# A seven-product block scheme for the second weight of two feed-forward layers

## The chip, the cores and the metric

One core of a Trainium2 chip runs the whole kernel as one program. The metric is the device time of one execution in microseconds. The kernel before took 1127.52 us (median of three runs, 1127.25 to 1127.96).

## What is computed

One layer of a streaming encoder for 512 tokens of width 1024, in float32: a feed-forward half step, a mixer (a recurrent branch and windowed attention), and a second feed-forward half step, with an RMS norm around each. The change touches the last product of the two feed-forward parts (FFNs).

```python
D_MODEL, SEQ, D_FF = 1024, 512, 2816

def rms_norm(x, g):
    y = x * lax.rsqrt(jnp.mean(x * x, axis=-1, keepdims=True) + RMS_EPS)
    return y * g

def swiglu(x, w1, w3, w2):
    return (jax.nn.silu(x @ w1) * (x @ w3)) @ w2

f = swiglu(rms_norm(h, ffn1_pre_g), ffn1_w1, ffn1_w3, ffn1_w2)
h = h + 0.5 * rms_norm(f, ffn1_post_g)
...                                    # the mixer
f = swiglu(rms_norm(h, ffn2_pre_g), ffn2_w1, ffn2_w3, ffn2_w2)
h = h + 0.5 * rms_norm(f, ffn2_post_g)
```

With `w2` the contraction runs over 2816 hidden channels, 22 tiles of 128. The result has 512 tokens (4 tiles of 128) by 1024 columns (2 halves of 512).

## The kernel before

**Numbers.** Every float32 operand is split into a high part (a copy to the matmul's float32r type) and a low part (what the copy lost). A product takes three matmuls: high by high, high by low, low by high. The copy to the high part runs on ACT (ScalarE), the subtraction for the low part on DVE (VectorE); `split2` (L211) is the pair. `split_dma` (L154) makes a low part without DVE: ACT writes the negated high part, and a transfer issued by POOL (GpSimd) adds the operand to it in place.

**Order.** The order of instructions on each engine is the order in which the program issues them; nothing is rearranged. `later(n, fn)` and `point()` (L197, L201) put a piece of work n steps further on. A list `order` (L102) holds the order in which weights are loaded; `dma_to`, `split_to` and `get` (L149, L164, L183) load, split and hand out the next ones. All weight loads go through SP's queue. Tiles in SBUF come from one pool of 42 equal slots of 4 KB per partition (`slot`, L63); the eight PSUM banks from another (`bank`, L67).

**w1 and w3** of an FFN already run in a seven-product block scheme (`Pairs`, L522), a job for two tiles of one weight, 84 matmuls of 256 columns each. At two places in its last job `Pairs.run` calls `tail()`, which prepares the start of what follows. In the first FFN the hidden tiles 2 and 3 are kept unscaled (`keep`, `gate_kept`, `swiglu_kept`) and finished after the jobs. `Hidden` holds the hidden tiles, and `Hidden.to` splits them.

**w2** runs in `tok_gemm` (L360, also used for `wo`): the tokens are the stationary operand, 512 columns of the weight are moving, and eight PSUM banks hold the whole result (four token tiles, two column halves). The first F = 15 contraction tiles go tile by tile over all tokens; the last RF = 7 are kept back and go token by token, so that each token tile is finished in turn, and its norm (`post_norm`, `norms`, L284, L308) runs while PE (TensorE) goes on. In the first FFN the tokens are then transposed (L331) for the mixer, while PE begins the next product on the first half of the tokens (L433 to L468). In the second FFN the result goes out. POOL has nothing to do in the w2 stages but to issue the loads of the norm gains and to scale one.

Of the kernel before, what the change touches and what calls it, by code (L numbers as in the profile page):

```python
# [51 lines left out]
def hybrid_layer(ctx: ExitStack, tc: tile.TileContext, a: dict, out: bass.AP):  # L52
# [50 lines left out]

    def want(name, n):
        order.extend((name, i) for i in range(n))

# [10 lines left out]
    want_ffn("w1a", "w3a", NC1)  # L117
    want("w2a", FT)
    order += [("xr", i) for i in range(8)]
# [14 lines left out]
    want_ffn("w1b", "w3b", NC2)  # L134
    want("w2b", FT)

# [146 lines left out]

    def post_norm(acc, t, gpost, scale, dst, after=None, last=False, eps=D * EPS, mid=None):  # L284

        ss = small(2, "ss")
        fg = slot([P, D], name="fg")
        junk = slot([P, D], name="junk")
        cs = [slice(n * 512, (n + 1) * 512) for n in range(2)]
        rs = Rstd2()  # L290
        for n, c in enumerate(cs):
            act.activation(junk[:, c], acc[n], AF.Square, accum_out=ss[:, n : n + 1])
            dve.scalar_tensor_tensor(out=fg[:, c], in0=acc[n], scalar=scale, in1=gpost[:, c], op0=ALU.mult, op1=ALU.mult)
            if n:
                rs.root(ss)
            else:
                rs.first(ss, eps)
        r = rs.value()
        if mid:
            mid()  # L300
        if last:
            cs = [slice(0, 512), slice(512, 768), slice(768, D)]
        for n, c in enumerate(cs):
            dve.scalar_tensor_tensor(out=dst[:, c], in0=fg[:, c], scalar=r, in1=h[t][:, c], op0=ALU.mult, op1=ALU.add)
            if after:
                after(n, c)

    def norms(acc, t, gpost, scale, gpre, spill, eps, mid=None):  # L308
# [12 lines left out]
        post_norm(acc, t, gpost, scale * NEWT, h[t], half, eps=eps, mid=mid)  # L321
# [37 lines left out]

    def tok_gemm(nm, xs, n, R, gpost_name, scale, gpre_name, first, x_to=None, xf=None, spill=False, then=None, eps=None):  # L360

# [11 lines left out]

        pre = min(2, F)
        x_to = x_to or (lambda k: None)
        for k in range(pre):
            x_to(k + 1)
            w[k] = get(nm, k, ahead=pre - k + 1)
        if pre:
            for tt in ((0, 1), (2, 3)):  # L380
                for k in range(pre):
# [4 lines left out]
        for k in range(pre, F):  # L386
            x_to(k + 2)
            w[k] = get(nm, k, ahead=2 + (R - 2) * (k + 1) // F)
            for t in range(NT):
                mm_tok(accs(t), xs[k], t, w[k], k == 0, False)  # L390
                if t % 2:
                    point()
        point(True)
        for k in range(F, n):
            x_to(k + 1)
            w[k] = get(nm, k, ahead=max(0, n - 1 - k), rawahead=2)
# [8 lines left out]
        for t in range(NT):  # L405
            for ns in ((0,), (1,)):
                for k in range(F, n):
                    mm_tok(accs(t), xs[k], t, w[k], k == 0, k == n - 1, ns)
            if not gpre_name:
                o = slot([P, D], name="o")  # L410

                def store(nn, c, t=t, o=o):
                    sp.dma_start(out=out[t * P : (t + 1) * P, c], in_=o[:, c])

                post_norm(acc[t], t, gpost, scale * NEWT, o, store, t == NT - 1)
# [8 lines left out]
            us[t] = norms(acc[t], t, gpost, scale, gpre, spill, ep(t))  # L424
            if t == 1:
                transpose_out(trs[t - 1], t - 1, xf)
# [19 lines left out]
        mm_feat(bs[0], ws[0], 0, 256, ks=range(3, KT))  # L446
        us[t] = norms(acc[t], t, gpost, scale, gpre, spill, ep(t), between)
        transpose_out(trs[t - 1], t - 1, parts=(1,))
# [24 lines left out]

    def silu_mul(ps1, ps3, t=None):

        t = t or slot([P, 2, SEQ], name="sw")
        act.activation(t[:, 0, :], ps1, AF.Silu)
        dve.tensor_tensor(out=t[:, 1, :], in0=ps3, in1=t[:, 0, :], op=ALU.mult)
        return t[:, 1, :]

    class Hidden:


        def __init__(self):
            self.f, self.t, self.done = [], {}, 0

        def to(self, n):
            while self.done < min(n, len(self.f)):
                assert self.f[self.done] is not None
                hT = slot([P, 2, SEQ], F32R, name="hT")  # L490
                split2(hT[:, 0, :], hT[:, 1, :], self.f[self.done])
                self.f[self.done] = None
                self.t[self.done] = hT
                self.done += 1

        def __getitem__(self, k):
            return self.t[k]

# [23 lines left out]
    class Pairs:  # L522
# [3 lines left out]
        def __init__(self, names, f0, f1, X, hid=None, R=None):  # L526
            self.R = R
            self.jobs = [(nm, f) for f in range(f0, f1, 2) for nm in names]
# [4 lines left out]
        def raws(self, m):  # L533
            k = self.k0 + 2 * len(self.jobs)
            dma_to(min(self.k0 + 2 * m + 2, k) + max(0, m + 1 - len(self.jobs)))

# [49 lines left out]
        def run(self, tail, hooks={}):  # L586
# [4 lines left out]
            for n, (nm, f) in enumerate(self.jobs):  # L591
# [48 lines left out]
                if not first:  # L640
                    c1 = self.c1[f]
                    dve.tensor_tensor(out=c1[:, 0, :], in0=c1[:, 0, :], in1=c[:, 0, :], op=ALU.mult)
                    dve.tensor_tensor(out=c1[:, 1, 256:], in0=c1[:, 1, 256:], in1=c[:, 1, 256:], op=ALU.mult)
                self.prep(n + 1, 4)
# [3 lines left out]
                def last(W=W, bu=bu, c=c, f=f, first=first):  # L648
# [9 lines left out]
                    else:  # L658
                        c1 = self.c1.pop(f)
                        dve.tensor_tensor(out=c1[:, 1, :256], in0=bu, in1=c1[:, 1, :256], op=ALU.mult)  # L660
                        self.hid.f += [c1[:, 0, :], c1[:, 1, :]]

# [178 lines left out]
    hid, X1 = Hidden(), {}  # L841
    hid.f = [None] * NC1
    Rb = slot([P, 2, SEQ], name="Rb")
# [162 lines left out]
    def swiglu(f):  # L1006
        t = gates.pop(f)
        hid.f[f] = silu_mul(t[:, 0, :], ps[2 * f + 1], t)

# [14 lines left out]
    def swiglu_kept(f):  # L1024
        t = kept.pop(f)
        dve.tensor_tensor(out=t[:, 1, :], in0=t[:, 0, :], in1=t[:, 1, :], op=ALU.mult)
        hid.f[f] = t[:, 1, :]

# [23 lines left out]
    for i in range(P // 16):  # L1052
        late[4 + i, 1] = [lambda i=i: bias_spread(i)]

    def w2_ahead():
        hid.to(hid.done + 1)
        split_to(st["split"] + 1)

    pairs_a.run(w2_ahead, late)
    X1 = pairs_a = late = None  # L1060
    for f in range(NG, NC1):
        later(1, lambda f=f: gate_kept(f))
        later(3, lambda f=f: swiglu_kept(f))
    later(10, softplus)
    xf = {(hh, th): slot([P, 4, 256], name="xf") for hh in range(2) for th in range(2)}
    bs = tok_gemm(
        "w2a", hid, FT, RF, "ffn1_post_g", 0.5, "mix_pre_g", [("xr", i) for i in range(4)], hid.to, xf=xf, spill=True, eps=veps)
    hid = None

# [391 lines left out]
    def operands():  # L1461
# [11 lines left out]
        "wo", mg, KT, RO, "mix_post_g", 1.0, "ffn2_pre_g",  # L1473
        [("w1b", 0), ("w3b", 0), ("w1b", 1), ("w3b", 1)], xf=xf, then=operands)


    dve.tensor_tensor(out=tn[3], in0=xf[1, 0], in1=tn[1], op=ALU.subtract)
    xf.clear()
    hid.f.append(silu_mul(bs[0], bs[1]))
    X2["t3"] = to_slots(tn[2])  # L1480
    hid.f.append(silu_mul(bs[2], bs[3]))
    del bs
    late = {(0, 1): [lambda: X2.update(t4=to_uT(tn[3], 0, 1)), tn.clear]}
    pairs_b.prep(1, 1)
    pairs_b.run(w2_ahead, late)
    X2 = pairs_b = None
    tok_gemm("w2b", hid, FT, RF, "ffn2_post_g", 0.5, None, [], hid.to)


# [23 lines left out]
BY_POOL = {("wg", i) for i in range(2, 8)} | {("wk", 0), ("wk", 1)}  # L1513
RF = 7
RO = 6

NC1 = 4
# [57 lines left out]
```

## Time and profile before

| | before |
|---|---|
| median of three runs | 1127.52 us |
| span of the profiled execution, first to last instruction | 1126.0 us |
| mean granted clock of TensorE | 0.998 |
| PE busy | 1117.5 us |
| DVE busy | 828.6 us |
| ACT busy | 620.2 us |
| POOL busy | 367.0 us |
| moved by DMA | 136.52 MB |

The profiled execution has no time of its own beside its span; the median of the runs is 1.5 us above it.

In the profile, a row of a group gives the source line, the engine, the operation, what is written and read, the count, and the shortest, median and longest duration in ns. A row in order of time gives the start and the duration in us, and in brackets how long the engine had been idle and what ended that. A row of a window gives for PE, PEld (weight loads), DVE, ACT and POOL the busy time and the number of instructions, then the granted clock, the DMA share and GB/s. Transfers have a size and the time from issue to landing.

### The profile page before, as it was taken

What the parts mean: (1) busy time and instruction counts of PE and PEld (TensorE: products, weight loads), DVE (VectorE), ACT (ScalarE), POOL (GpSimd) and SP (SyncE); (2) the same over time, 40 slices, a digit from 0 to 9 for tenths busy, and PEclk for the clock granted to TensorE, in tenths of its full rate; (3) what the DMA queues carried; (4) which work ended last, traced back from release to release, by engine and by line L of the source; (5) the groups of instructions that cost most, each with busy time, mean ns of one, the idle gap of its engine ahead of it and who ended that gap; (6) DMA issues with size and microseconds to landing.
All of it is one profiled execution on the core that took longest, in us unless ns stands there. A gap on an engine that the chain in (4) does not pass through costs nothing. (4 is left out here: it accounts for less than half of the span.)

```text
span 1126.0 us, 17883 instructions
## 1 busy us (share of the span) xinstructions
PE 1117.5 (99%) x6946; PEld 1008.3 (90%) x6946; DVE 828.6 (74%) x1225; ACT 620.2 (55%) x1107; POOL 367.0 (33%) x284
## 2 busy tenths in 40 slices
PE   9999999999999999999999999999999999999997
PEld 7899999988889877899888888889999999998886
DVE  5889989886436978887768867767897877975313
ACT  7755555574336678666655654456455555564211
POOL 0044444200101423242656663011765566700000
PEclk9999999999999999999999999999999999999999
DMA  9226563265214543156122336421333232265101
GB/s 346 100 82 149 132 133 113 76 224 166 97 62 153 149 117 101 38 173 239 59 92 75 131 112 225 179 103 40 111 108 102 92 113 86 88 201 170 37 20 56
DMA packets 40309, 136.52 MB, mean 121 GB/s; under 512 B 4880, under 2 KB 6800, under 8 KB 40224
## 3 DMA queue, kind: packets, MB, share of 16 engines
q1 hardware_dynamic: 36432, 123.28, 32.3%
q0 software_dynamic: 3504, 11.58, 5.2%
q8 instruction: 54, 0.88, 0.3%
q10 hardware_dynamic: 288, 0.52, 0.1%
q14 instruction: 31, 0.25, 0.1%
HBM read 121.74 MB, written 11.53 MB: 118 GB/s over the span
## 5 line engine op out<-in xcount | busy, mean ns | idle before, releaser
L517 PE MATMUL c<-uT,wlo 128*128 128x256 f32 x516 | 146.3, 283 | 0.0
L518 PE MATMUL c<-uT,whi 128*128 128x256 f32 x516 | 146.3, 283 | 0.0
L516 PE MATMUL c<-uT,whi 128*128 128x256 f32 x516 | 146.3, 283 | 0.0
L516 PE MATMUL c<-Xh,whi 128*128 128x256 f32 x504 | 143.0, 284 | 0.0
L517 PE MATMUL c<-Xh,wlo 128*128 128x256 f32 x504 | 143.0, 284 | 0.0
L242 PE MATMUL acc<-whi,hT 128*128 128x512 f32 x352 | 137.3, 390 | 0.0
L243 PE MATMUL acc<-wlo,hT 128*128 128x512 f32 x352 | 137.1, 390 | 0.0
L244 PE MATMUL acc<-whi,hT 128*128 128x512 f32 x352 | 137.1, 390 | 0.0
L224 PE MATMUL f<-uT,whi 128*128 128x512 f32 (+1 forms) x368 | 136.6, 371 | 0.0
L225 PE MATMUL f<-uT,wlo 128*128 128x512 f32 (+1 forms) x368 | 135.0, 367 | 0.0
L226 PE MATMUL f<-uT,whi 128*128 128x512 f32 (+1 forms) x368 | 135.0, 367 | 0.0
L214 DVE TENSOR_TENSOR wlo<-S,whi 128x1024 fp32r<-128x1024 f32 x86 | 125.2, 1456 | 7.4 <-ACT whi L213 3.5
L518 PE MATMUL c<-Xl,whi 128*128 128x256 f32 x456 | 129.3, 284 | 0.0
L213 ACT ACTIVATE whi<-S 128x1024 fp32r<-128x1024 f32 x86 | 88.3, 1054 | 23.1 <-DVE S L563 22.0
L516 PEld LDWEIGHTS c<-uT,whi 128*128 128x128 f32 x516 | 99.2, 192 | 0.2
L517 PEld LDWEIGHTS c<-uT,wlo 128*128 128x128 f32 x516 | 99.2, 192 | 0.2
L518 PEld LDWEIGHTS c<-uT,whi 128*128 128x128 f32 x516 | 99.2, 192 | 0.0
L516 PEld LDWEIGHTS c<-Xh,whi 128*128 128x128 f32 x504 | 96.9, 192 | 0.3 <-issue 0.3
L517 PEld LDWEIGHTS c<-Xh,wlo 128*128 128x128 f32 x504 | 96.9, 192 | 0.1
L518 PEld LDWEIGHTS c<-Xl,whi 128*128 128x128 f32 x456 | 87.7, 192 | 0.0
L224 PEld LDWEIGHTS f<-uT,whi 128*128 128x128 f32 x368 | 69.5, 189 | 12.5 <-issue 1.7
L226 PEld LDWEIGHTS f<-uT,whi 128*128 128x128 f32 x368 | 69.4, 189 | 11.4
(383 smaller groups left out, 2855.4 us busy)
## 6 DMA issues: line engine op xcount, KB each, us to landing
raw_w2a<-in_w2a_dram SPq DMA_DIRECT2D x22, 512.0 KB, 4.2
raw_w1b<-in_w1b_dram SPq DMA_DIRECT2D x22, 512.0 KB, 4.1
raw_w3b<-in_w3b_dram SPq DMA_DIRECT2D x22, 512.0 KB, 4.3
raw_w2b<-in_w2b_dram SPq DMA_DIRECT2D x22, 512.0 KB, 4.3
raw_w3a<-in_w3a_dram SPq DMA_DIRECT2D x21, 512.0 KB, 4.4
raw_w1a<-in_w1a_dram SPq DMA_DIRECT2D x20, 512.0 KB, 4.3
raw_wg<-in_wg_dram SPq DMA_DIRECT2D x16, 512.0 KB, 3.8
raw_xr<-in_xr_dram SPq DMA_DIRECT2D x8, 512.0 KB, 3.9
```

The source lines that it names most:

```text
L213: act.activation(hi, src, AF.Copy)
L214: dve.tensor_tensor(out=lo, in0=src, in1=f32(hi), op=ALU.subtract)
L224: pe.matmul(ps[:, c0:c1], wh[:, s], h_, start=k == 0 and c0 == 0, stop=False, skip_group_check=True)
L225: pe.matmul(ps[:, c0:c1], wl[:, s], h_, start=False, stop=False, skip_group_check=True)
L226: pe.matmul(ps[:, c0:c1], wh[:, s], l_, start=False, stop=k == KT - 1, skip_group_check=True)
L242: pe.matmul(acc[n], x[:, 0, c], wh[:, s], start=first, stop=False)
L243: pe.matmul(acc[n], x[:, 0, c], wl[:, s], start=False, stop=False)
L244: pe.matmul(acc[n], x[:, 1, c], wh[:, s], start=False, stop=last)
L516: pe.matmul(ps, wh[:, s], xh, start=first, stop=False, skip_group_check=True)
L517: pe.matmul(ps, wl[:, s], xh, start=False, stop=False, skip_group_check=True)
L518: pe.matmul(ps, wh[:, s], xl, start=False, stop=k == 3, skip_group_check=True)
```

## The change

For both FFNs, the first SF = 16 of the 22 contraction tiles of `w2` leave `tok_gemm`'s order and run in a new class `Halves`. It takes four groups of four contraction tiles (index i). In each group the tiles 0 and 2 form one half of the contraction, 1 and 3 the other. With two halves of the tokens (256 each) and two of the columns (512 each), the product has the form of a two by two block matrix product. It is done with seven block products (m1, m5, m6, m2, m7, m3, m4) in place of eight. Each product runs over the four groups. One product of one group is a unit `u`, 28 in all, with 12 matmuls of 128 by 512.

The operands are sums of blocks that are made in place, step by step, behind the preparation of each unit (`sums`): those of the weight blocks on POOL, those of the x blocks on DVE, and four on POOL. Units are prepared four ahead (`prep`). The low parts of 12 weight blocks per FFN (`LO_DMA`: groups 1 and 3 of all products but m1) come from ACT and a transfer that POOL issues.

The results of the products are gathered in four SBUF tiles (`out`). The last six contraction tiles go token by token as before (RF = 6), and `post_norm` first adds the gathered part to them (`part`). Beside this: the hidden tiles 0 to 15 are written to eight slots that hold the block layout (`place`); the kept tiles 2 and 3 are finished inside the pair jobs 12 to 15; h is dropped before the block part and loaded again at unit 12, from the input in the first FFN, from DRAM scratch in the second, for which the stage after `wo` stores it; the weight blocks are loaded in rows of 2 KB, not 4 KB.

```diff
-    def post_norm(acc, t, gpost, scale, dst, after=None, last=False, eps=D * EPS, mid=None):
+    def post_norm(acc, t, gpost, scale, dst, after=None, last=False, eps=D * EPS, mid=None, part=None):
...
+        if part:
+            for n, o in enumerate(part):
+                dve.tensor_tensor(out=o, in0=acc[n], in1=o, op=ALU.add)
+            acc = part
...
+    class Halves:
...
+        GS = (1, 2, 3, 0)
+        LOADS = (("b11", 0), ("b11", 1), ("b12", 0), ("b11", 2), ("b12", 1), ("b11", 3), ("b12", 2), ("b12", 3),
+                 *((b, i) for b in ("b22", "b21") for i in range(4)))
+        PRODUCTS = (("b11", 0, 0), ("b12", 0, 1), ("b12", 0, 1), ("b21", 1, 0), ("b11", 0, 0), ("b22", 1, 0), ("b21", 1, 1))
+        NAMES = ("m1", "m5", "m6", "m2", "m7", "m3", "m4")
...
+        def sums(self, m, i):
+
+            T = lambda o, p, q, op, e=pool: e.tensor_tensor(out=self.raw[o, i], in0=self.raw[p, i], in1=self.raw[q, i], op=op)
+            S = lambda o, p, q, op, e: e.tensor_tensor(out=self.x(i, *o), in0=self.x(i, *p), in1=self.x(i, *q), op=op)
+            if m == "first":
+                T("b12", "b12", "b11", ALU.subtract)
+                S((0, 1), (0, 1), (1, 1), ALU.add, dve)
+            elif m == "m5":
+                T("b12", "b22", "b12", ALU.subtract)
+                S((0, 1), (0, 1), (0, 0), ALU.subtract, dve)
+            elif m == "m6":
+                T("b11", "b12", "b11", ALU.subtract)
+                S((0, 0), (1, 1), (0, 1), ALU.subtract, dve)
+            elif m == "m2":
+                S((1, 0), (1, 0), (0, 1), ALU.subtract, pool)
+                T("b21", "b21", "b12", ALU.subtract)
+
+        def prep(self, n):
+
+            while self.ready < min(n, 28):
+                u = self.ready
+                self.ready += 1
+                m, i = u // 4, u % 4
+                self.load(min(u + 9, 16))
+                b, odd, half = self.PRODUCTS[m]
+                hi, lo = (slot([P, 2, 512], F32R, name=x) for x in ("whi", "wlo"))
+                if u < 3:
+                    xs = slot([P, 2, 2, 256], F32R, name="hx")
+                else:
+                    xs = uT[:, :, (u + 1) % 8, :].rearrange("p e (j c) -> p e j c", j=2)
+                src = self.raw[b, i]
+                act.activation(hi, src, AF.Copy)
+                if (m, i) in LO_DMA:
+                    act.activation(lo, src, AF.Copy, scale=-1.0)
+                    pool.dma_start(out=lo, in_=src, accum_op=ALU.add)
+                xsrc = self.x(i, odd, half)
+                act.activation(xs[:, 0, :, :], xsrc, AF.Copy)
+                if (m, i) not in LO_DMA:
+                    dve.tensor_tensor(out=lo, in0=src, in1=f32(hi), op=ALU.subtract)
+                dve.tensor_tensor(out=xs[:, 1, :, :], in0=xsrc, in1=f32(xs[:, 0, :, :]), op=ALU.subtract)
+                self.ops[u] = hi, lo, xs
+                self.sums(self.NAMES[m], i)
+                if m == 0:
+                    self.sums("first", i)
+
+        def unit(self, u):
+            m = u // 4
+            key = "bu" if self.NAMES[m] in ("m1", "m6", "m7", "m4") else "bx" if self.NAMES[m] in ("m5", "m3") else "bc"
...
+            for j in range(2):
+                for t, ps in enumerate(self.bank[key]):
+                    c = slice(t * P, (t + 1) * P)
+                    first = start and j == 0
+                    pe.matmul(ps, xs[:, 0, j, c], hi[:, j, :], start=first, stop=False, skip_group_check=True)
+                    pe.matmul(ps, xs[:, 0, j, c], lo[:, j, :], start=False, stop=False, skip_group_check=True)
+                    pe.matmul(ps, xs[:, 1, j, c], hi[:, j, :], start=False, stop=u % 4 == 3, skip_group_check=True)
+
+        def out(self, m):
+
+            copy, add = {"m1": ("q1", "bu"), "m5": ("q5", "bx"), "m6": ("u", "bu"), "m4": ("v", "bu")}, {
+                "m2": ("q1", "bc"), "m7": ("q5", "bu"), "m3": ("u", "bx")}
...
+        def run(self):
+            for u in range(28):
+                self.prep(u + 4)
+                for fn in self.hooks.get(u, ()):
+                    fn()
+                self.unit(u)
+                if u % 4 == 3:
+                    later(2, lambda m=self.NAMES[u // 4]: self.out(m), 0)
+                point()
...
+    for f in range(NG, NC1):
+        late[12 + 2 * (f - NG), 3] = [lambda f=f: gate_kept(f)]
+        late[13 + 2 * (f - NG), 3] = [lambda f=f: swiglu_kept(f)]
...
+    h.clear()
+    half = Halves("w2a", hid, tail_hooks(hid))
+    half.hooks.setdefault(12, []).append(lambda: h_load([a["x"][t * P : (t + 1) * P, :] for t in range(NT)]))
+    pairs_a.more = half.load
+    pairs_a.run(lambda: half.prep(half.ready + 1), late)
...
-RF = 7
+SF = 16
+RF = FT - SF
 RO = 6
+
+LO_DMA = {(m, i) for m in range(1, 7) for i in (1, 3)}
```

`tail_hooks` puts the splitting of the six hidden tiles and weight tiles that are left at the units 16, 18, 20, 22, 24 and 26. In `out`, ACT copies the banks of m1, m5, m6 and m4 to the four tiles, and DVE adds those of m2, m7 and m3.

More of the change, by code (lines that the diff above doesn't have):

```diff
@@ L102, in hybrid_layer, with want @@
     order = []
-    def want(name, n):
-        order.extend((name, i) for i in range(n))
+    def want(name, n, first=0):
+        order.extend((name, i) for i in range(first, n))
     paired = set()
@@ L306, in post_norm, with norms @@
                 after(n, c)
-    def norms(acc, t, gpost, scale, gpre, spill, eps, mid=None):
+    def norms(acc, t, gpost, scale, gpre, spill, eps, mid=None, part=None):
         hg = slot([P, D], name="hg")
@@ L319, in half @@
                 dve.tensor_tensor(out=hg[:, c], in0=h[t][:, c], in1=gpre[:, c], op=ALU.mult)
[L321 removed]
+        post_norm(acc, t, gpost, scale * NEWT, h[t], half, eps=eps, mid=mid, part=part)
         ht = h[t]
@@ L385, in tok_gemm @@
                             point()
[L386 to L392, printed above, removed]
+            for k in range(both, F):
+                x_to(k + 2)
+                w[k] = get(nm, k, ahead=2 + (R - 2) * (k + 1) // F)
+                for t in range(NT):
+                    mm_tok(accs(t), xs[k], t, w[k], k == 0, False)
+                    if t % 2:
+                        point()
         point(True)
+        part = pre.part if pre else lambda t: None
         for k in range(F, n):
@@ L423, in tok_gemm @@
                 transpose_out(trs[t - 1], t - 1)
-            us[t] = norms(acc[t], t, gpost, scale, gpre, spill, ep(t))
+            us[t] = norms(acc[t], t, gpost, scale, gpre, spill, ep(t), part=part(t))
             if t == 1:
@@ L446, in tok_gemm @@
         mm_feat(bs[0], ws[0], 0, 256, ks=range(3, KT))
-        us[t] = norms(acc[t], t, gpost, scale, gpre, spill, ep(t), between)
+        us[t] = norms(acc[t], t, gpost, scale, gpre, spill, ep(t), between, part(t))
         transpose_out(trs[t - 1], t - 1, parts=(1,))
@@ L1066, in hybrid_layer @@
     bs = tok_gemm(
-        "w2a", hid, FT, RF, "ffn1_post_g", 0.5, "mix_pre_g", [("xr", i) for i in range(4)], hid.to, xf=xf, spill=True, eps=veps)
-    hid = None
+        "w2a", hid, FT, RF, "ffn1_post_g", 0.5, "mix_pre_g", [("xr", i) for i in range(4)], hid.to, xf=xf, spill=True, eps=veps, pre=half)
+    hid = half = None
     def rg_load():
@@ L1484, in hybrid_layer @@
     pairs_b.prep(1, 1)
-    pairs_b.run(w2_ahead, late)
+    half = Halves("w2b", hid, tail_hooks(hid))
+    half.hooks.setdefault(12, []).append(lambda: h_load([h_scr[t] for t in range(NT)]))
+    pairs_b.more = half.load
+    pairs_b.run(lambda: half.prep(half.ready + 1), late)
     X2 = pairs_b = None
-    tok_gemm("w2b", hid, FT, RF, "ffn2_post_g", 0.5, None, [], hid.to)
+    tok_gemm("w2b", hid, FT, RF, "ffn2_post_g", 0.5, None, [], hid.to, pre=half)
 CONV_AT = (0, 1, 2, 4, 5, 6, 8, 10)
```

121 lines of the change are left out of this document (82 added, 39 removed).

## The prediction, made before the changed kernel was run

> **What bounds the kernel now.** I read the shares of the page first, then the waits of PE, then the order in time where the w2 stages begin and end.
>
> ```profile
> span 1126.0 us, 17883 instructions
> PE 1117.5 (99%) x6946; PEld 1008.3 (90%) x6946; DVE 828.6 (74%) x1225; ACT 620.2 (55%) x1107; POOL 367.0 (33%) x284
> ...
> PE w L820 <- POOL warm L817: 1.1, 1, 1.1
> PE f L224 <- DVE o L1384: 0.3, 1, 0.3
> ...
> 232.08 0.40 PE L242 MATMUL acc<-whi,hT 128*128 128x512 f32 x1
> ...
> 999.23 0.40 PE L242 MATMUL acc<-whi,hT 128*128 128x512 f32 x1
> ...
> 1118.71 0.39 PE L244 MATMUL acc<-whi,hT 128*128 128x512 f32 x1
> ```
>
> PE waits 1.4 us in all. Whatever takes matmuls away shortens the run, as long as PE stays fed. The first w2 stage starts at 232.08. The second has 22 x 4 x 2 x 3 = 528 matmuls whose starts run from 999.23 to 1118.71, so (1118.71 - 999.23) / 527 = 0.2267 us each. Matmul ends are modelled, hence the longer 0.39; the spacing is what counts.
>
> **The gain.** Sixteen of the 22 tiles take 16 x 24 = 384 matmuls now, 87.05 us per FFN. The new scheme has 7 products x 4 groups x 12 = 336 of the same shape, 76.2 us (a unit, one product of one group, is 12 matmuls or 2.72 us). That is 10.9 us per FFN, 21.8 us in all, if nothing waits.
>
> **What feeds the units.** Each unit needs a weight block and an x block split into high and low parts. Per FFN that is 28 weight splits instead of 16 and 28 x splits instead of 16, plus the sums of blocks: 12 on DVE (128x512), 4 on POOL (128x512) and 16 on POOL (128x1024). Of the weight low parts, 12 are made by ACT and an accumulating transfer that POOL issues.
>
> ```profile
> L178 ACT ACTIVATE whi<-raw_w2a x22: 1042/1044/1062, 228.3 to 282.5; 128x1024 fp32r<-128x1024 f32 x22
> L179 DVE TENSOR_TENSOR wlo<-raw_w2a,whi x22: 1215/1222/1227, 229.3 to 284.0; 128x1024 fp32r<-128x1024 f32 x22
> ...
> L213 ACT ACTIVATE hT<-cc x38: 612/622/634, 242.0 to 1054.7; 128x512 fp32r<-128x512 f32 x38
> L214 DVE TENSOR_TENSOR hT<-cc,hT x38: 677/686/694, 243.5 to 1055.5; 128x512 fp32r<-128x512 f32 x38
> ...
> L1194 POOL TENSOR_TENSOR xf<-xf,xf x4: 2412/3259/3278, 363.8 to 373.0; 128x1024 f32<-128x1024 f32 x4
> ...
> 363.82 12.44 POOL L1194 TENSOR_TENSOR xf<-xf,xf 128x1024 f32<-128x1024 f32 x4 [9.24 <-ACT xf L357]
> ...
> 370.59 3.41 DVE L1083 TENSOR_TENSOR rglo<-rgraw,rghi 128x1024 fp32r<-128x1024 f32 x1
> ...
> 383.94 1.22 DVE L179 TENSOR_TENSOR wlo<-raw_xr,whi 128x1024 fp32r<-128x1024 f32 x1
> ...
> 973.56 1.30 POOL L567 TENSOR_TENSOR S<-raw_w3b 128x512 f32<-128x512 f32 x1 [1.92 <-PE c L518]
> ...
> L161 POOL DMA_DIRECT2D wlo<-xf x4: 861/870/978, 380.1 to 395.0; - x4
> ...
> DMA to landing us min/median/max: 4.5/6.3/9.7
> ```
>
> A weight split is 1.05 us on ACT and 1.22 on DVE, an x split 0.62 and 0.69. A POOL sum of 128x1024 takes 2.41 alone and 3.26 beside DVE; one of 128x512 takes 1.30. While POOL works on its four sums, the DVE split that takes 1.22 alone takes 3.41: the two engines take turns (POOL's four take 12.44), and each POOL sum holds such a DVE operation up by 2.2 us. Issuing an accumulating transfer occupies POOL for 0.87, and it lands 4.5 to 9.7 later.
>
> **POOL's queue is the longest.** ACT has (28 x 1.67) + (12 x 1.05) + 4.8 of copies + 10 for the last six tiles = 74 us, DVE (16 x 1.22) + (46 x 0.69) + (6 x 1.91) = 63, both under PE's 76.2. POOL has waits. Its order is fixed, per FFN (T a 128x1024 sum, S a 128x512 sum, D a transfer; the digit is the block index i):
> - first: T0 T1 T2 T3
> - m5: T0, D1 T1, T2, D3 T3
> - m6: T0, D1 T1, T2, D3 T3
> - m2: S0 T0, D1 S1 T1, S2 T2, D3 S3 T3
> - then D1 of m7, and five more transfers
>
> In m5 the sum overwrites `b12`, in m2 `b21`, and in both that block is what the transfer just issued reads. So T1 and T3 wait for its landing, with all of POOL's later work behind them: four waits for a landing per FFN. In m6 the sum writes `b11`, which nobody is reading, so it doesn't wait.
>
> ```profile
> wlo<-xf POOLq DMA_DIRECT2D x1, 512.0 KB, 4.5
> ...
> wlo<-xf POOLq DMA_DIRECT2D x1, 512.0 KB, 6.6
> ```
>
> These two are the transfers of this kind that were issued alone (at 380.11 and 390.97). The new ones are alone too, since POOL stands still behind them; I take the middle, 5.5, and keep 4.5 and 6.6. A T gets 2.5 (bounds 2.41 and 3.26), near the lower end, because DVE catches up while POOL waits.
>
> From the start of m5's T0 to the landing of m7's D1, which PE's unit 17 (counted from 0) needs:
> - m5: 2 x 2.5 + 2 x (5.5 + 2.5) = 21.0
> - m6: 4 x 2.5 + 2 x 0.87 = 11.7
> - m2: 2 x (1.3 + 2.5) + 2 x (5.5 + 2.5) = 23.6, the other two S under the landings
> - D1 of m7: 5.5
> - sum 61.8 us (with 2.41 and 4.5: 55.7; with 3.26 and 6.6: 76.5)
>
> **When m5's T0 starts.** It waits until DVE has made the low part of unit 4, behind the splits of units 0 to 3 and what is left of the pair jobs.
>
> ```profile
> 229.34 1.23 DVE L179 TENSOR_TENSOR wlo<-raw_w2a,whi 128x1024 fp32r<-128x1024 f32 x1 [0.25 <-ACT whi L178]
> 230.49 0.42 DVE L629 TENSOR_TENSOR cc<-c,ct 128x256 f32<-128x256 f32 x1
> ...
> 234.29 0.42 DVE L660 TENSOR_TENSOR cc<-c,cc 128x256 f32<-128x256 f32 x1
> 234.62 2.35 DVE L179 TENSOR_TENSOR wlo<-raw_w2a,whi 128x1024 fp32r<-128x1024 f32 x2
> ```
>
> The first split starts at 229.34, which is 2.7 before PE's first w2 matmul. Four units are 4 x (1.22 + 0.69 + 0.69) = 10.4, the six leftovers of the pair jobs about 2.8, unit 4's low part 1.2, less some 1.7 because operations follow each other 0.09 closer than they last (two take 2.35). That gives +10.0 after PE's start. The four first T run in the same time and hold DVE 2.2 each. None to all of them may hit; I count two, as the blocks of the first two are loaded before the pair jobs end: +14.4 (bounds +10.0 and +18.8). The same queue stands at 999.23, so I use it for both FFNs.
>
> **The sum.** Unit 17 can start at 14.4 + 61.8 = +76.2, where an unhindered PE would be at 17 x 2.72 = +46.2. Eleven units are left, 11 x 2.72 = 29.9, so the block part ends at +106.1 instead of +87.05: 19.1 us lost per FFN, 38.2 in all, the 21.8 already in it. For these last units ACT has 27.1 us of work (7 units at 1.67, 4 negated copies at 1.05, 6 hidden and weight tiles at 1.67, copies 1.2) against 29.9 on PE: a thin cover, and were it gone the loss grows by the difference.
>
> **The ends.** The partial sums are added before the norms: two more DVE operations of 0.69 per token tile, of which the second comes after the last matmul.
>
> ```profile
> 1119.14 0.60 ACT L292 ACTIVATE junk<-acc 128x512 f32<-128x512 f32 x1 [4.07 <-PE acc L244]
> ...
> 1119.86 0.69 DVE L293 SCALAR_TENSOR_TENSOR fg<-acc,bc_ffn_post_g 128x512 f32<-128x512 f32 x1 [4.01 <-ACT junk L292]
> ```
>
> The square at 1119.14 will start one addition later: +0.7 at the end of the kernel, 0.5 after the first FFN, where PE's half-token matmuls cover a part (bounds 0 and 1.4 together for each). I take 1.2.
>
> At nothing I put: the reload of h (four transfers per FFN, due only at the norms, some 100 us later; the DMA engines were 0.54 busy at 235 to 280 below; uncovered, one landing); the spill after wo; the kept gates moved into the pair jobs (0.7 us of DVE in each of four jobs of 9.6 us; uncovered, 2.6); half-length rows of the w2 loads (inside the bounds of T0's start).
>
> ```profile
> 235.00:280.00 45.00, 45.00 (x200) 37.28 (x200) 35.67 (x64) 25.74 (x34) 0.00 (x0) 1.00 0.54 176
> ...
> 1120.00:1121.00 1.00, 0.00 (x0) 0.00 (x0) 0.89 (x3) 0.15 (x1) 0.00 (x0) 1.00 0.00 0
> 1121.00:1122.00 1.00, 0.00 (x0) 0.00 (x0) 0.85 (x3) 0.00 (x0) 0.00 (x0) 0.64 0.00 0
> 1122.00:1123.00 1.00, 0.00 (x0) 0.00 (x0) 0.95 (x3) 0.00 (x0) 0.00 (x0) 0.50 0.00 0
> ```
>
> PE's last matmul ends at 1119.1, and the granted clock (the column before the DMA share) falls to 0.50 some two microseconds later. Stalls of 5 us will bring that into the block part; while POOL sets the pace it costs nothing, and after the last stall it costs half of however long the clock stays low, which no row shows. I add nothing. By the Trainium skill (TensorE: Matmul & The Clock Gate, part 1) the full clock comes back after about 3.4 us of work; an estimate from that page is 1.7 us more per FFN and a time of 1170.
>
> The span becomes 1126.0 + 38.2 + 1.2 = 1165.4. The median of the runs, 1127.52, is 1.5 above the span; so **1167 us**.
>
> The Trainium skill (DMA: Bandwidth & Descriptors, anatomy of one DMA) has a transfer issued from GpSimd at 2.0 us plus its bytes over 436 GB/s, an estimate of 3.2 us for 512 KB, which would shorten five landings by 2.3 each and give 1144; the rows say 4.5 and more.
>
> **Rivals.**
> - *A shorter POOL chain.* Landings 4.5, T 2.41, start +10.0: unit 17 at +65.7, end +95.6, loss 8.5 per FFN, time 1127.5 + 17.1 + 1.2 = 1146. For it: the transfer at 380.11. Against it: the others, and the sums beside DVE.
> - *PE stays fed.* If m7's D1 lands by +46.2 the gain is whole: 1127.5 - 21.8 + 1.2 = 1107. It decides at +57.1, where nothing is lost or won. For it: units are prepared four ahead, 10.9 us of PE. Against it: the 33 us of sums and issues alone, with a start of +10, leave 14 us for five landings at break-even, 2.8 each; no accumulating transfer in the trace lands that soon.
> - *Turns between POOL and DVE throughout, and crowded transfers.* T 3.26, landing 6.6, start +18.8: 18.8 + 76.5 + 29.9 = +125.2, loss 38.1 per FFN, time 1127.5 + 76.3 + 1.2 = 1205. For it: 3.26 is the median of the row. Against it: POOL's waits leave DVE free time.
>
> **How the numbers follow.** Forecast 0.62, shorter chain 0.20, PE fed 0.07, crowded 0.11. About 0.2% can be told from no change here. The shorter chain includes 0.03 in which it ends within that bound. So slower 0.90, same 0.03, faster 0.07. The range runs from 1135, below the short chain, to 1205, the crowded one; what is left out is PE fed and the worst mixtures of the bounds.
>
> **What would show it.** PE waits of 3 to 6 us in front of the units with transferred low parts in m5, m6 and m2, and the longest total put down to those landings; POOL idle between issue and sum four times per FFN; the block parts near 106 us instead of 76. If POOL's sums of m2 are done by +50, or DVE or ACT and not POOL comes last before PE's waits, the argument is wrong.

## The result, and the profile after

The changed kernel takes 1175.9 us (median of four runs, 1174.3 to 1177.0) against 1127.6 beside it: a ratio of 1.0426, with an interval of 1.0412 to 1.0441. It is slower by 48.3 us. The forecast was 1167, with a range of 1135 to 1205.

From the page of the changed kernel:

```profile
span 1174.1 us, 18020 instructions
...
PE 1116.1 (95%) x6850; PEld 1000.4 (85%) x6850; DVE 941.8 (80%) x1301; ACT 685.0 (58%) x1195; POOL 480.1 (41%) x348
...
PEclk9999999997899999999999999999999999988899
```

PE's share falls from 99% to 95%, and the granted clock dips in two places, at a quarter and near the end of the span: the two w2 stages. PE's busy time has hardly fallen although it has 96 matmuls fewer, since a matmul at half clock counts for longer. The waits of PE (total, count, longest) say what it stands for:

```profile
PE hw L599 <- DMA wlo<-raw_w2a: 24.0, 6, 8.2
PE hw L599 <- DMA wlo<-raw_w2b: 22.0, 5, 7.8
PE w L954 <- POOL warm L951: 1.1, 1, 1.1
```

Before, the longest total was 1.1 us. Now 46 us go to transferred low parts of w2. PE's instructions in order of time give the block parts (L598 to L600 are the units, L242 begins the token-by-token tail):

```profile
232.86 0.40 PE L598 MATMUL hw<-whi,hx 128*128 128x512 f32 x1
...
307.07 0.80 PE L599 MATMUL hw<-wlo,uT 128*128 128x512 f32 x1 [8.25 <-DMA wlo<-raw_w2a]
...
345.50 0.39 PE L242 MATMUL acc<-whi,hT 128*128 128x512 f32 x1
...
1026.46 0.40 PE L598 MATMUL hw<-whi,hx 128*128 128x512 f32 x1
...
1133.76 0.39 PE L242 MATMUL acc<-whi,hT 128*128 128x512 f32 x1
```

The first block part takes 345.50 - 232.86 = 112.6 us, the second 1133.76 - 1026.46 = 107.3, where the sixteen tiles took 87.05 before. That is 25.6 + 20.2 = 45.8 of the 48.1 us by which the span has grown. The other 2.3 lie at the start of the first block part (0.8 later than before) and behind the additions of the partial sums.

POOL's instructions of the first block part in order of time (start, duration; in brackets the idle time before and what ended it; x2 are two of a kind without a gap between them):

```profile
245.31 2.78 POOL L544 TENSOR_TENSOR raw_w2a<-raw_w2a,raw_w2a 128x1024 f32<-128x1024 f32 x1 [11.78 <-DVE wlo L580]
248.03 0.94 POOL L576 DMA_DIRECT2D wlo<-raw_w2a  x1
252.60 5.46 POOL L544 TENSOR_TENSOR raw_w2a<-raw_w2a,raw_w2a 128x1024 f32<-128x1024 f32 x2 [3.63 <-DMA wlo<-raw_w2a]
258.02 0.86 POOL L576 DMA_DIRECT2D wlo<-raw_w2a  x1
262.51 5.26 POOL L544 TENSOR_TENSOR raw_w2a<-raw_w2a,raw_w2a 128x1024 f32<-128x1024 f32 x2 [3.63 <-DMA wlo<-raw_w2a]
267.72 0.84 POOL L576 DMA_DIRECT2D wlo<-raw_w2a  x1
268.32 4.93 POOL L544 TENSOR_TENSOR raw_w2a<-raw_w2a,raw_w2a 128x1024 f32<-128x1024 f32 x2
272.92 1.16 POOL L576 DMA_DIRECT2D wlo<-raw_w2a  x1
273.51 2.97 POOL L544 TENSOR_TENSOR raw_w2a<-raw_w2a,raw_w2a 128x1024 f32<-128x1024 f32 x1
279.46 1.29 POOL L545 TENSOR_TENSOR hEO<-hEO,hEO 128x512 f32<-128x512 f32 x1 [2.98 <-DVE z L1090]
...
283.04 0.85 POOL L576 DMA_DIRECT2D wlo<-raw_w2a  x1
288.45 2.16 POOL L545 TENSOR_TENSOR hEO<-hEO,hEO 128x512 f32<-128x512 f32 x1 [4.57 <-DVE uT L581]
291.50 2.50 POOL L544 TENSOR_TENSOR raw_w2a<-raw_w2a,raw_w2a 128x1024 f32<-128x1024 f32 x1 [0.88 <-DMA wlo<-raw_w2a]
...
298.52 0.87 POOL L576 DMA_DIRECT2D wlo<-raw_w2a  x1
...
307.09 2.37 POOL L544 TENSOR_TENSOR raw_w2a<-raw_w2a,raw_w2a 128x1024 f32<-128x1024 f32 x1 [6.41 <-DMA wlo<-raw_w2a]
309.40 0.84 POOL L576 DMA_DIRECT2D wlo<-raw_w2a  x1
```

Four sums wait for a landing: T1 and T3 of m5 (252.60 and 262.51) and of m2 (291.50 and 307.09). In m6 (from 265 to 276.5) there is no such wait. The transfers ahead of them land after 252.60 - 248.03 = 4.6 and 4.5 us in m5, but after 8.5 and 8.6 in m2. The windows of these four stretches, and of the one behind the last stall (busy time of PE, PEld, DVE, ACT and POOL with counts, granted clock, DMA share, GB/s):

```profile
248.10:252.60 4.50, 1.36 (x7) 0.79 (x5) 4.43 (x7) 1.58 (x2) 0.87 (x2) 1.00 0.59 117
258.10:262.50 4.40, 1.82 (x9) 1.17 (x8) 4.40 (x6) 1.58 (x2) 0.78 (x1) 1.00 0.60 119
283.10:291.50 8.40, 2.92 (x14) 2.09 (x12) 7.71 (x30) 4.84 (x7) 2.95 (x3) 0.80 0.85 225
298.60:307.00 8.40, 0.22 (x1) 0.00 (x0) 4.37 (x4) 2.52 (x3) 2.08 (x2) 0.69 0.80 187
...
307.10:312.00 4.90, 4.90 (x12) 3.84 (x13) 0.90 (x2) 2.50 (x4) 4.01 (x3) 0.50 0.27 53
```

The long landings fall into stretches in which the DMA engines are 0.80 to 0.85 busy, with the reload of h or the tail's weight loads beside them. At the first of them POOL's next instruction, a sum of x blocks, waits 4.57 us for DVE anyway and starts at 288.45. Only 0.88 us of idle time is left there that the landing ends. In the last window PE runs at half clock for 4.9 us, which loses half of them.

Some rows of DVE's instructions in the same stretch are worth a second look:

```profile
262.62 2.89 DVE L581 TENSOR_TENSOR uT<-hEO,uT 128x512 fp32r<-128x512 f32 x1
265.43 2.90 DVE L545 TENSOR_TENSOR hEO<-hEO,hEO 128x512 f32<-128x512 f32 x1
268.25 8.79 DVE L581 TENSOR_TENSOR uT<-hEO,uT 128x512 fp32r<-128x512 f32 x1
```

The third takes 8.79 us for an operation that takes 0.69 alone. It lasts as long as POOL's four instructions from 268.32 to 276.5 (three sums and an issue), which follow each other without a gap. The two rows before it take 2.89 and 2.90: each waits through one sum of POOL's pair from 262.51. The second FFN has the same pattern, with 8.82 us.

### The profile page after: what moved, and what is told of

Its sections match the earlier page's. It is cut to its first block, busy times and chain, and to the rows that moved or that the text cites. A ratio compares the mean times of both kernels' runs of the same rounds, so it can differ in the third digit from the quotient of the medians.

```text
span 1174.1 us, 18020 instructions
## 1 busy us (share of the span) xinstructions
PE 1116.1 (95%) x6850; PEld 1000.4 (85%) x6850; DVE 941.8 (80%) x1301; ACT 685.0 (58%) x1195; POOL 480.1 (41%) x348
## 4 chain that ended last, share of the span: by engine, by line
PE 76%; DVE 8%; issue 6%; POOL 5%; DMA 3%; ACT 2%; SPq 0%; DVEq 0%; POOLq 0%; ACTq 0%
PE c L648 11%; PE c L649 11%; PE c L647 11%; PE f L224 8%; PE f L225 8%; PE f L226 8%; PE acc L243 3%; PE acc L244 3%; PE acc L242 3%; POOL raw_w2b L544 2%; DVE uT L581 1%; PE hw L599 1%; PE hw L600 1%; PE hw L598 1%; DVE wlo L580 1%
## 5 line engine op out<-in xcount | busy, mean ns | idle before, releaser
L599 PE MATMUL hw<-wlo,uT 128*128 128x512 f32 x200 | 86.4, 432 | 46.0 <-DMA wlo<-raw_w2a 24.0
L214 DVE TENSOR_TENSOR wlo<-S,whi 128x1024 fp32r<-128x1024 f32 x86 | 117.7, 1369 | 5.9 <-POOL OL L1530 3.1
L599 PEld LDWEIGHTS hw<-wlo,uT 128*128 128x128 f32 x200 | 41.3, 207 | 59.4 <-DMA wlo<-raw_w2a 26.5
L649 PEld LDWEIGHTS c<-Xl,whi 128*128 128x128 f32 x456 | 87.5, 192 | 0.0
L600 PE MATMUL hw<-whi,uT 128*128 128x512 f32 x200 | 84.0, 420 | 0.0
L598 PE MATMUL hw<-whi,uT 128*128 128x512 f32 x200 | 83.1, 416 | 0.0
L224 PEld LDWEIGHTS f<-uT,whi 128*128 128x128 f32 x368 | 69.4, 189 | 13.1 <-issue 1.4
```

What stands on the lines that cost most here:

```text
L214: dve.tensor_tensor(out=lo, in0=src, in1=f32(hi), op=ALU.subtract)
L224: pe.matmul(ps[:, c0:c1], wh[:, s], h_, start=k == 0 and c0 == 0, stop=False, skip_group_check=True)
L598: pe.matmul(ps, xs[:, 0, j, c], hi[:, j, :], start=first, stop=False, skip_group_check=True)
L599: pe.matmul(ps, xs[:, 0, j, c], lo[:, j, :], start=False, stop=False, skip_group_check=True)
L600: pe.matmul(ps, xs[:, 1, j, c], hi[:, j, :], start=False, stop=u % 4 == 3, skip_group_check=True)
L649: pe.matmul(ps, wh[:, s], xl, start=False, stop=k == 3, skip_group_check=True)
```

## The experiments

Two theories were to be told apart. **Landings**: POOL's queue is late because four sums per FFN wait for a landing, as the prediction had it. **Exclusion**: POOL's sums are dear wherever they stand, because POOL's sums and DVE's operations on two tiles in SBUF don't run at the same time. A third, **the work**: 28 splits and the sums are too much for any arrangement. "Block" is the length of the two block parts, read as above; without any stall they would take 28 x 2.72 = 76.2.

| run | what differs from the changed kernel | time, us | ratio to before | blocks, us |
|---|---|---|---|---|
| changed kernel | | 1175.9 | 1.0426 | 112.6, 107.3 |
| e1_fresh | no sum overwrites a block under transfer | 1169.0 | 1.0365 | 110.4, 102.7 |
| e2_hlate | h loaded 15 units later | 1175.1 | 1.0419 | 112.3, 105.3 |
| e3_both | both | 1171.0 | 1.0383 | 111.8, 102.2 |
| e4_nodma | no transfers, DVE makes all low parts | 1161.4 | 1.0297 | 106.4, 99.1 |
| e5_fill | matmuls put into the stalls | 1182.4 | 1.0486 | 113.7, 112.4 |
| e10_nosums | weight sums left out | 1111.8 | 0.986 | 77.8, 76.6 |
| e11_dve | all sums on DVE | 1129.8 | 1.0025 | 90.2, 82.7 |
| e13_dve_dma | and 18 transfers | 1128.5 | 1.0010 | 86.0, 84.9 |
| e14_late_all | and sums of m2 done later | 1130.2 | 1.0023 | 88.1, 87.5 |
| e15_late_odd | the same with 12 transfers | 1123.2 | 0.9962 | 84.6, 84.5 |
| e17_eight | the same with 8 transfers | 1128.0 | 1.0002 | 86.0, 85.1 |
| e16_spare_sums | e15 and idle sums on POOL | 1184.9 | 1.0508 | 110.5, 110.3 |

### Take the waits for landings away (e1_fresh)

```diff
+                if m in ("m5", "m2") and i % 2:
+                    self.raw[o, i] = slot([P, 2, 512], name="sum")
                 pool.tensor_tensor(out=self.raw[o, i], in0=x, in1=y, op=op)
```

> Only the write target of eight POOL sums changes (m5 and m2, blocks 1 and 3, both FFNs): a new tile, so that they need not wait for the transfer that reads the old one. If POOL's queue with its waits for a landing sets the pace: the 32 us in which POOL waited for a landing before such a sum go to nearly zero, m7's first transfer is issued some 12 to 15 us earlier in each block, and the time falls by 20 to 30 us, to 1146 to 1156. If DVE and POOL taking turns sets the pace, or PE's clock, the time stays within 5 us of 1176.

The ratio is 1.0365 (1.0334 to 1.0395): 7 us less, far short of 20. POOL's waits for landings are gone from its list, but PE has a new first line, and DVE and POOL show why:

```profile
PE hw L604 <- DVE uT L585: 18.8, 2, 9.7
```

```profile
257.13 14.24 DVE L585 TENSOR_TENSOR uT<-hEO,uT 128x512 fp32r<-128x512 f32 x1
```

```profile
257.23 2.62 POOL L548 TENSOR_TENSOR sum<-raw_w2a,raw_w2a 128x1024 f32<-128x1024 f32 x1
...
267.63 3.19 POOL L548 TENSOR_TENSOR raw_w2a<-sum,raw_w2a 128x1024 f32<-128x1024 f32 x1
```

One DVE operation stood for 14.24 us, while POOL did five sums and two issues without a gap (257.23 to 270.8). The landings that POOL no longer waits for had been DVE's time to work.

### Move the reload of h (e2_hlate, e3_both)

```diff
-    half.hooks.setdefault(12, []).append(lambda: h_load(...))
+    half.hooks.setdefault(27, []).append(lambda: h_load(...))
```

> Only the reload of h moves, from unit 12 to unit 27. If its four transfers of 512 KB crowd the two accumulating transfers of m2 (8.4 and 8.5 us to landing in the first FFN, 8.2 and 6.3 in the second, against 4.4 to 4.7 in m5 and m6), these land in about 4.5 and the time falls by 10 to 14 us, to 1162 to 1166. If something else makes them long (POOL or DVE at work beside them), they stay above 8 and the time stays within 3 us of 1176.

> e1 and e2 together. If POOL's waits for landings are the cause, a landing matters only to the matmuls that read it once POOL does not wait for it; the units are prepared four ahead, so the reload is worth less here than alone: 0 to 6 us below e1, 1142 to 1154. If the two are independent costs, the full 10 to 14 below e1.

No change: 1175.1, and 1171.0 for both edits together, which is not below the first edit alone. Yet the reload is what had made the first landing of m2 long in the first FFN: without it that transfer, issued at 283.59, lands after 4.4 us, with the DMA engines no busier than in m5. POOL gains nothing by it, since its next sum waits for DVE, until 289.02 here and until 288.45 in the changed kernel. The last landing of m2 stays long; POOL's rows of e2_hlate have it at 8.3 us, with the tail's weight loads beside it. The window of the first landing, then POOL's rows:

```profile
283.60:288.00 4.40, 0.30 (x2) 0.00 (x0) 3.76 (x25) 4.31 (x6) 0.84 (x2) 0.76 0.60 119
```

```profile
289.02 2.19 POOL L545 TENSOR_TENSOR hEO<-hEO,hEO 128x512 f32<-128x512 f32 x1 [4.58 <-DVE uT L581]
...
298.93 0.86 POOL L576 DMA_DIRECT2D wlo<-raw_w2a  x1
...
307.19 2.36 POOL L544 TENSOR_TENSOR raw_w2a<-raw_w2a,raw_w2a 128x1024 f32<-128x1024 f32 x1 [6.12 <-DMA wlo<-raw_w2a]
```

### Take the transfers away (e4_nodma)

```diff
-LO_DMA = {(m, i) for m in range(1, 7) for i in (1, 3)}
+LO_DMA = set()
```

> No accumulating transfers: all 28 low parts of weight blocks per FFN by DVE. If the landings are the cause, POOL has no such waits and DVE 12 x 1.22 = 14.6 us more per FFN. What DVE and POOL cannot do at the same time in the first 16 units is then 16 x 2.2 + 4 x 1.1 of POOL and 16 x 1.91 + 12 x 0.69 of DVE, 78 us, of which some 10 come before PE starts: unit 16 at about +67, a loss of 13 us per FFN, 1154 (1145 to 1165). If DVE's own time is what PE waits for, it gets worse than 1176.

1161.4, 14.5 us less, inside the range named. No transfer is left to be waited for, but the stalls are, now for DVE:

```profile
PE hw L599 <- DVE wlo L580: 21.4, 13, 4.2
PE hw L600 <- DVE uT L581: 8.5, 6, 2.3
```

So doing without the transfers and their landings, at the price of 14.6 us more of DVE per FFN, wins back less than a third of the loss.

### Leave the weight sums out (e10_nosums)

```diff
-            T = lambda o, p, q, op, e=pool: e.tensor_tensor(out=self.raw[o, i], in0=self.raw[p, i], in1=self.raw[q, i], op=op)
+            T = lambda o, p, q, op: None
```

> The sixteen sums of weight blocks per FFN are left out (the result is therefore not the reference's); the transfers, the splits and the x sums stay. If those sums on POOL (with the waits in POOL's queue and the DVE operations that they hold) are the cost, PE is fed but for the first units and the time is 1105 to 1118 us, below the kernel before. If the accumulating transfers' own landings or ACT and DVE splitting 28 blocks instead of 16 are as large a cost, the time stays above 1130 and PE's waits are still put down to the landings or the splits.

1111.8 us, a ratio of 0.986 (0.9831 to 0.9889), with blocks of 77.8 and 76.6. PE's waits in the units are gone but for this:

```profile
PE hw L599 <- DMA wlo<-raw_w2a: 0.8, 2, 0.5
```

Twelve transfers, 28 splits of weights and of x, the x sums, the reload of h and the additions at the end all fit under PE. The 64 us hang on the 16 weight sums per FFN alone.

### Put work into the stalls (e5_fill)

```diff
+            for _ in range(FILL.get(u, 0)):
+                pe.matmul(self.fill, self.old[1][:, 0, 0, :P], self.old[0][:, 0, :], start=True, stop=True)
```

> Before units 5, 7, 9, 13 and 15 PE gets 12, 10, 14, 22 and 26 matmuls into a bank that nobody reads (84 per FFN, 19 us at 0.2267 each), placed where PE stands still. If PE only waits there, they cost nothing, and by keeping the granted clock up after the last stall they save up to 2.5 us per FFN: 1170 to 1176 us. If PE's own work decides anywhere in the block part, each matmul costs its 0.2267 and the time rises by up to 38 us.

1182.4: neither expectation. Of some 38 us of added matmuls 6.5 show, so most of them did run in stalls, but nothing was saved. The filling matmuls read the operands of the unit before and so keep its buffers for longer, and new waits of 3 to 4 us stood at later units; that the one causes the other is likely but not shown. What the half clock alone costs is therefore read from the window above, not from this run.

### The same sums on DVE (e11_dve, e13_dve_dma)

```diff
-            T = lambda o, p, q, op, e=pool: e.tensor_tensor(out=self.raw[o, i], in0=self.raw[p, i], in1=self.raw[q, i], op=op)
+                if m in ("m5", "m2") and i % 2:
+                    self.raw[o, i] = slot([P, 2, 512], name="sum")
+                dve.tensor_tensor(out=self.raw[o, i], in0=x, in1=y, op=op)
...
-                S((1, 0), (1, 0), (0, 1), ALU.subtract, pool)
+                S((1, 0), (1, 0), (0, 1), ALU.subtract, dve)
```

In the second, beside this, a fresh buffer for all of m5 and m2 and `LO_DMA` with all blocks of m5, m6 and m2.

> All sums of blocks go to DVE (a 128x1024 sum at 1.22, a 128x512 sum at 0.69), those of m5 and m2 that would overwrite a block under transfer go to a fresh buffer, and POOL only issues the transfers. DVE then has about 54 us of work for the first sixteen units (10 splits of weights, 16 sums of weights, 16 splits and 12 or so sums of x, some 2.8 of pair jobs), where POOL needed 76. If the cost is POOL's sums holding DVE for longer than DVE would need for the same sums, unit 17 can start near +55 and the time is 1115 to 1135 us. If DVE's own amount of work is the limit in any case, the time stays at 1160 or above.

> As with all sums on DVE, but the low parts of all blocks of m5, m6 and m2 are made by transfer (18 transfers per FFN instead of 12), which takes 6 x 1.22 = 7.3 us per FFN from DVE and gives 6 x 1.05 to ACT. If DVE's amount of work is what remains, the time falls by 5 to 15 us against the kernel with all sums on DVE. If crowded landings are what remains (eighteen of 4.4 to 8.5 us, each prepared four units or 10.9 us ahead), it does not fall, or rises by up to 10.

1129.8 us: 39 us less than with the same fresh buffers and the sums on POOL (e1_fresh). Nothing was taken away here. DVE does the sums as well as all that it did, and is done earlier. The rows of DVE's x splits in the window 225 to 330 (busy, mean ns) show what it was spared, first in the changed kernel, then with the sums on DVE:

```profile
L581 DVE TENSOR_TENSOR uT<-hEO,uT 128x512 fp32r<-128x512 f32 x23 | 30.6, 1340 | 9.6 <-ACT uT L578 9.6
```

```profile
L585 DVE TENSOR_TENSOR uT<-hEO,uT 128x512 fp32r<-128x512 f32 x25 | 16.8, 683 | 1.9 <-ACT uT L582 1.8
L548 DVE TENSOR_TENSOR raw_w2a<-raw_w2a,raw_w2a 128x1024 f32<-128x1024 f32 x10 | 12.2, 1216 | 0.0
```

But DVE is now full. In the window from the block part's start to the time at which an unhindered PE would reach unit 16 (the columns as above), it is busy for 42.85 of 43.5 us and late by one wait of PE of 4.8 us:

```profile
233.00:276.50 43.50, 38.92 (x160) 28.96 (x158) 42.85 (x69) 32.26 (x45) 5.23 (x6) 1.00 0.61 147
```

Six more transfers per FFN gave only 1.3 us, less than the 5 that were named for DVE's work and within the spread of the runs (1128.1 to 1132.5 without them, 1126.9 to 1130.4 with them).

### What is left: DVE's work or landings (e14_late_all, e15_late_odd, e17_eight)

The sums of m2 are moved behind unit 16 and on, and in the first FFN a chain of small DVE operations (softplus) 14 steps later. The three differ only in the blocks whose low part is transferred (18, 12 and 8 per FFN).

```diff
-                self.sums(self.NAMES[m], i)
+                if m != 3:
+                    self.sums("m2" if m == 4 else self.NAMES[m], i)
...
-    later(10, softplus)
+    later(24, softplus)
```

> All sums on DVE, transfers for all of m5, m6 and m2, and two pieces of DVE work moved past unit 16: the sums of m2 (per FFN 4 x 1.22 + 4 x 0.69 = 7.6 us, needed only from units 20 and 24 on) and in the first FFN the softplus chain (some 5 us). If what still delays unit 16 and 17 is DVE's amount of work ahead of them, the block parts fall from 86.0 and 84.9 to 77 to 80 us and the time to 1110 to 1118 us. If it is the landings of the transfers, the time stays within 3 us of 1128.

> As before this one, but only the odd blocks have their low part made by transfer (12 per FFN instead of 18), so DVE has 7.3 us more and ACT 6.3 us less per FFN. DVE's work ahead of unit 16 is then again close to the time that PE gives it. If DVE's amount of work decides, 1114 to 1124 us and slower than the kernel with all of m5, m6 and m2 by transfer; if crowded transfers or ACT decide, it is the faster of the two.

> All sums on DVE and the late ones moved, and the low parts of m3 and m4 are made by DVE (8 transfers per FFN instead of 12): 4.9 us more of DVE and 4.2 us less of ACT per FFN, after unit 16. If the crowded landings of m3 and m4 (PE's waits at units 21 and 27) are what remains, the time falls by 2 to 6 us to 1117 to 1121. If DVE's amount of work is, it rises by 2 to 10.

With 18 transfers 1130.2, with 12 it is 1123.2, with 8 it is 1128.0. Both limits are there, close to each other. With 18, PE waits for landings. With 12, less; the waits of PE in the two kernels, in this order:

```profile
PE hw L604 <- DMA wlo<-raw_w2b: 6.4, 4, 3.1
PE hw L604 <- DMA wlo<-raw_w2a: 5.6, 3, 2.4
```

```profile
PE hw L604 <- DMA wlo<-raw_w2a: 2.6, 2, 1.4
PE hw L604 <- DMA wlo<-raw_w2b: 2.2, 1, 2.2
PE hw L604 <- DVE wlo L584: 2.1, 2, 1.5
```

With 8, the first line is DVE's. The forecast that moving DVE's work alone would bring 77 to 80 per block was wrong. The version with 12 transfers is below both kernels: 1123.2 us, a ratio of 0.9962 (0.9949 to 0.9975) to the kernel before, so 0.4% less.

### Sums on POOL that nobody waits for (e16_spare_sums)

```diff
+                if u < 16:
+                    pool.tensor_tensor(out=self.spare, in0=self.spare, in1=self.spare, op=ALU.subtract)
```

> The kernel with all sums on DVE and the late ones moved, in which POOL only issues transfers, and beside it POOL does sixteen 128x1024 sums per FFN on a spare buffer that nobody reads, one with each of units 0 to 15. No result and no wait for a landing depends on them; only a transfer behind one in POOL's queue is issued up to 2.5 us later. If POOL's arithmetic itself holds DVE up (2.2 us for each), DVE loses up to 35 us per FFN and the time rises by 30 to 60 us, to 1153 to 1183. If POOL's cost was only its own length in the chain of results and landings, the time rises by less than 8, to 1131 at most.

1184.9, 61.7 us more than without them, above the range named, and not by the way that was named. Here it is POOL that stood still. POOL's queue in order of time, the window beside it, and PE:

```profile
257.61 26.66 POOL L590 TENSOR_TENSOR spare<-spare 128x1024 f32<-128x1024 f32 x1
...
286.18 0.85 POOL L582 DMA_DIRECT2D wlo<-sum  x1
```

```profile
257.70:282.60 24.90, 13.53 (x58) 10.20 (x56) 24.82 (x31) 14.98 (x20) 24.90 (x2) 0.84 0.11 21
```

```profile
290.63 0.79 PE L608 MATMUL hw<-wlo,uT 128*128 128x512 f32 x1 [19.24 <-DMA wlo<-sum]
```

One sum took 26.66 us; the next, with DVE idle, took 1.89. In 24.90 us of these DVE did 31 operations, was busy for 24.82, and none was held. Then DVE ran dry, POOL finished, and the transfer queued behind the two sums was issued at 286.18; PE had waited 19.24 us for it. So a sum that nobody reads costs one such stall in each FFN: the block parts are 26 us longer than without them. The first starts 5.5 us later, too.

## Why the prediction came out as it did

**The gate.** That POOL's in-order queue decides was right: PE's long waits are for transferred low parts, POOL waits for a landing exactly four times in the first FFN, and T3 of m2 starts at 307.09 - 232.86 = +74.2 (the test named was +50). The gain of 21.8 us is real too: without the sums it is there but for 6 us of it, the ends and small waits.

**Its terms.** First FFN, forecast and profile:
- m5's T0 starts at +12.4 instead of +14.4 (in the second FFN earlier still).
- m5 takes 19.8 instead of 21.0 (245.31 to the middle of the pair at 262.51), m6 11.4 instead of 11.7.
- **m2 takes 33 instead of 23.6** (276.5 to 309.4). This is the mis-sized term. Its start waits 3.0 for DVE, in the second FFN too: DVE has just been shut out for 8.8. Then its two landings take 8.5 and 8.6 instead of 5.5. Behind the first, POOL's next sum waits for DVE, busy with the softplus chain, so the length of that landing shows only in part. "Alone" was true of POOL's queue, but not of the DMA engines, which were 0.80 to 0.85 busy. The two rows that 5.5 was taken from weren't alone, either: POOL issued its next transfers at 382.95 and 393.82, before they had landed, and SP had loads under way. The reload of h and the weight loads were put at nothing where they come beside these landings; moving the reload alone (e2_hlate) brought the first of them to 4.4 and the time nowhere.
- The last long stall is at unit 15, whose low part is m2's D3, and not at unit 17: D1 of m7 takes 4.4 instead of 5.5 and has landed at 313.8, while PE, at half clock, gets to unit 17 only at 314.7. From D3's landing, 155 matmuls at 0.2267 are 35.1, where the forecast had 29.9 after unit 17.
- **The half clock** after the last stall was put at nothing. It is 4.9 us at 0.50 in the first FFN, some 2.4 lost. The Trainium skill (TensorE: Matmul & The Clock Gate, part 1) has the full clock back after about 3.4 us of work, and the estimate from it was 1.7. The trace is nearer to that than to nothing, though the stretch is longer here.
- The ends and the later start are 2.3 in place of 1.2.

Sum: 45.8 + 2.3 = 48.1 against 39.4 forecast. Of the 8.7 the first FFN has 6.5 (25.6 lost, not 19.1), the second 1.1, the ends 1.1. In the first, +74.2, 35.1, 2.4 and a late wait of 0.8 at unit 25 make up 112.5 of the 112.6. In the second the early start (+9.7 instead of +14.4) and the long m2 nearly cancel, which is luck.

**The mechanism, as the runs have it.** The prediction counted the hold of DVE by POOL only at the start (two times 2.2) and T at 2.5 "because DVE catches up while POOL waits". That clause holds the larger part of the truth. The waits for landings and the exclusion of the two engines are two hurdles in one chain. Taking the first away (e1_fresh) gives 7 us, since POOL then shuts DVE out for 14 us at a stretch. Moving the sums, which takes the second away, gives 39 more. So of the 64 us between the changed kernel and the one without weight sums, 46 are due to the sums' place on POOL and the waits that come with it (e11_dve). The other 18 stay with the sums on DVE; they are DVE's time and the landings together, and no run parts the two. The statement that DVE stays under PE's time was right for DVE's own list and left out the time for which POOL's sums keep it waiting. With the sums as work of its own DVE is as long as PE: 42.85 of 43.5 us up to unit 16.

**The rivals.** *A shorter chain* needed landings of 4.5; m5 has them, m2 not. *PE stays fed* needed the sums to vanish, and e10_nosums at 1111.8 is its size. *Turns throughout and crowded transfers* was right about m2's landings, and wrong about T, which takes 2.4 to 3.4.

## What to carry to other kernels

Work given to POOL is not free because POOL is idle: where DVE works on two tiles in SBUF, a POOL sum of 2.4 us held a DVE operation up by some 2.2, and a string of them by 8 to 14, so a sum of 1.22 us on DVE was cheaper than one of 2.4 beside it. When a queue waits, ask who works in that time before taking the wait away. And price a landing by the transfers that will be under way beside it. The DMA share alone doesn't tell: it was 0.80 in the window of the landing of 8.5 us (298.60 to 307.00), and 0.80 in that of the 4.5 us in the kernel before (380.10 to 384.60).

## What the runs showed that was not expected

The two engines exclude each other, and the turns that the prediction read are only one form of it. In the kernel before, POOL's four sums run without a gap and one DVE operation comes in behind each (the one of 1.22 us that lasts 3.41 is one of them). The pair of sums from 262.51 in the changed kernel lets DVE in the same way. But from 268.25 a DVE operation waits through four POOL instructions (8.79 us), in e1_fresh through seven (14.24 us), and in e16_spare_sums a POOL sum waits through 31 DVE operations (26.66 us).

What decides between turns and a shut-out no run tests. The traces differ in one point, which may as well be an effect as a cause. Where a DVE operation comes in between two POOL sums, the second sum starts at most 0.05 us before the first has ended: in the pair from 262.51, 264.92 against 262.51 + 2.44 = 264.95. Where it stays out, the second starts 0.28 us or more before: in the string from 268.32, 270.63 against 268.32 + 2.62 = 270.94.

The Trainium skill (SBUF — State Buffer, "Who interferes with whom") says that a DVE instruction with two SBUF inputs contends with a GpSimd instruction that reads SBUF; of DVE's two-port modes it says that whoever issues first gets the shared ports for the whole instruction and the other blocks. The runs agree with the first, show such blocking for operations with two inputs, and add that it can last over a string of instructions. That it is these ports, and not something else that both need, no run here shows by itself.
